# Final norm spread over the last two experts, its row loads on GpSimd's queue, the last six way-down quarters unsplit

## The chip, the cores and the metric

The kernel runs as one program on one core of a Trainium2 chip. The metric is the device time of an execution in microseconds; three runs of the kernel before are at hand, and one more execution was profiled. The engines are TensorE (PE), VectorE (DVE), ScalarE (ACT), GpSimd (POOL) and SyncE (SP, which only issues transfers). Each takes its instructions strictly in the order in which the scheduler has put them.

## The reference

Two transformer blocks on a sequence of 1024 rows of 1024 float32 numbers. Only the end of the second block matters here: 16 experts, each of which takes 128 rows, and a root-mean-square norm of the whole result.

```python
xs = jax.vmap(lambda hb, ib: hb[ib])(h, idx)                 # 128 rows for each expert
a = jnp.einsum('becd,edf->becf', xs, w_gate)
u = jnp.einsum('becd,edf->becf', xs, w_up)
y = jnp.einsum('becf,efd->becd', jax.nn.silu(a) * u, w_down) * g[..., None]
flat = (idx + (jnp.arange(bsz) * n)[:, None, None]).reshape(-1)
out = jax.ops.segment_sum(y.reshape(-1, d), flat, num_segments=bsz * n)
...
x = x + gt2 * out
return rmsnorm_2(x, g_final)     # x * rsqrt(mean(x*x) + EPS) * g_final, row by row
```

A row can be taken by several experts or by none.

## The kernel before

**Quarters.** Each expert's 1024 hidden columns are worked off in four quarters of 256, so there are 64 quarters, here numbered 0 to 63; expert 13 ends with quarter 55, expert 14 with 59, expert 15 with 63. A quarter q has three weight tiles of 1 MB: two with gate and up columns (gu q a and gu q b) and one of way-down rows (wd q). `pipelined` runs three stages, one step apart: `ex_gu(q)` (24 products into `pg`, then SiLU and a multiply into `sg`), `ex_T(q)` (two transposes into `pT`, copied out) and `ex_down(q)` (products into `py`, which collects the four quarters of an expert). So wd q is used two steps after gu q.

**Split weights.** The products run on pairs of float32r numbers: ACT casts half a tile (`wh`, line 1521), DVE subtracts (`wl`, line 1522), and `mm3` makes three products of each pair (lines 187 to 189). `wh` and `wl` have four buffers each, so the split is at most two tiles ahead of PE. Only the very last way-down quarter, 63, is multiplied unsplit (line 1739): four float32 products straight from the loaded tile, without a cast or a subtraction.

**Loads.** SP issues all weight loads in an order of its own queue, each as soon as the slot that it goes to is free. `raw_tile` hands out 17 slots of 1 MB in a fixed turn over six pools, so that a load runs up to 17 tiles ahead of its use. A split tile's slot is free when DVE has made its second `wl`.

**The end of an expert.** After its last quarter ACT scales `py` into `ys` (line 1745), POOL multiplies by a row (1746) and issues an indirect DMA that adds the 128 rows into `x3_d` in HBM (1750). For expert 14 DVE does both steps in one (1748), and all loads that are left are asked for there, the last three (wd 61, 62 and 63) behind POOL copies that read its `ys` (1498). Then `final_rows` loads the norm's weights `gfin` (1761), gathers expert 15's 128 rows (`xg`, 1763), loads all of `x3_d` into four slots of the same ring (`x3t`, two row tiles of 512 KB each, line 1770, on SP), and norms the eight row tiles: sum of squares on ACT (168), `vrstd` on DVE (161), a power on POOL (164), a scaling on DVE (1775) and a store to `out` on SP (1776). Expert 15's rows are added to `xg` in SBUF, normed on their own (lines 1786 to 1793), and put over the stored ones by an indirect DMA (1794).

**Order.** A list scheduler with its own estimate of times decides the order on each engine, so an instruction can stand ahead of one that was written before it. Tiles of one pool are placed in the order in which they are asked for.

Of the kernel before, what the change touches and what calls it, by code (L numbers as in the profile page):

```python
# [17 lines left out]
P = 128  # L18
# [45 lines left out]
LASTN = 3  # L64
# [30 lines left out]
def tile_two_blocks(ctx, tc, A, out):  # L95
# [51 lines left out]
    def trow(t):  # L147
        return slice(t * P, (t + 1) * P)
# [1490 lines left out]
    with TP(name="exg", bufs=2, space=PSUM) as psg, \  # L1639
# [69 lines left out]
        def ex_T(i, ac):  # L1709
            whole = i == 4 * NE - 1  # L1710
# [12 lines left out]
        def ex_down(i, a):  # L1723
            e, c4 = divmod(i, 4)
            whole = i == 4 * NE - 1
# [16 lines left out]
            if c4 == 3 and e < NE - 1:  # L1742
                ys = ex.tile([P, D], F32, name="ys", tag="xs", bufs=XSB)
                if e < NE - 2:
                    nc.scalar.activation(ys, py, AF.Copy, scale=xT[e][3])
                    nc.gpsimd.tensor_tensor(out=ys, in0=ys, in1=gt2, op=ALU.mult)
                else:
                    nc.vector.scalar_tensor_tensor(out=ys, in0=py, scalar=xT[e][3], in1=gt2,
                                                   op0=ALU.mult, op1=ALU.mult)
                nc.gpsimd.indirect_dma_start(out=x3_d, out_offset=bass.IndirectOffsetOnAxis(ap=xT[e][2], axis=0),  # L1750
                                             in_=ys, in_offset=None, compute_op=ALU.add)
                if e == NE - 2:
                    while order:
                        fetch(nc.sync, ys if len(order) <= LASTN else None)
                    final_rows()

        def final_rows():

            i_ = ROWS.index("g_final_2")
            last["g"] = ex.tile([P, D], F32, name="gfin", tag="xs", bufs=XSB)  # L1760
            nc.sync.dma_start(last["g"], A["rows"][i_:i_ + 1, :].partition_broadcast(P).rearrange("p o n -> p (o n)"))
            last["x"] = ex.tile([P, D], F32, name="xg", tag="xs", bufs=XSB)
            nc.gpsimd.indirect_dma_start(out=last["x"], out_offset=None, in_=x3_d,
                                         in_offset=bass.IndirectOffsetOnAxis(ap=xT[NE - 1][2], axis=0))
            for u in range(NT // 2):
                xt = raw_tile("x3t")
                for j in range(2):
                    t = 2 * u + j
                    x3 = xt[:, j * D:(j + 1) * D]
                    nc.sync.dma_start(x3, x3_d[trow(t), :])  # L1770
# [137 lines left out]
```

## Time and profile before

| | us |
|---|---|
| median of three runs (2452.44 to 2456.56) | 2456.46 |
| the profiled execution | 2458.82 |
| its span, first to last instruction | 2456.8 |
| PE busy over the span | 2329.6 |
| DVE busy over the span | 1609.7 |
| ACT busy over the span | 1123.5 |

A view groups or lists instructions of that one execution; times are counted from its first instruction. 2.0 us of the execution lie outside the span. Ends of matmuls are modelled, so the starts of PE's rows are the better clock. Idle time in square brackets stands with the engine and the operation that ended it.

### The profile page before, as it was taken

How to read it: one execution, taken by the hardware profiler on the slowest of the kernel's cores; microseconds unless marked ns; L12 is line 12 of the kernel's file. 1: busy time of each engine (PE TensorE's matmuls, PEld its weight loads, DVE VectorE, ACT ScalarE, POOL GpSimd, SP SyncE). 2: the span in 40 equal slices, each digit the busy share in tenths (PEclk: the TensorE clock that was granted, in tenths of full speed). 3: DMA queues.
4: the chain of work that ended last, by engine and by line, in shares of the span. 5: the costliest groups of instructions: out<-in, count | busy, mean ns of one | idle time of the engine just before them, and what ended most of it. 6: DMA issues, size and time to landing. Idle time of an engine off the chain costs nothing. (4 is left out here: it accounts for less than half of the span.)

```text
span 2456.8 us, 33997 instructions
## 1 busy us (share of the span) xinstructions
PE 2329.6 (95%) x12876; PEld 1876.7 (76%) x12876; DVE 1609.7 (66%) x2566; ACT 1123.5 (46%) x1933; POOL 606.6 (25%) x604
## 2 busy tenths in 40 slices
PE   7999999999999999999997999999959999999996
PEld 7977787787878878788876978666737888877774
DVE  4265666457686665454557742575377999999887
ACT  4254565343321222222223421453237887877775
POOL 1100540130000000000006400263164565565512
PEclk9999899999999999999998999999979999999998
DMA  5111003225243332111115220014778999999975
GB/s 199 30 48 57 24 27 99 97 99 162 83 156 103 120 103 65 47 52 43 52 54 144 88 64 26 26 40 144 236 286 335 383 381 379 397 361 366 367 256 214
DMA packets 111031, 381.66 MB, mean 155 GB/s; under 512 B 12215, under 2 KB 19224, under 8 KB 94484
## 3 DMA queue, kind: packets, MB, share of 16 engines
q1 hardware_dynamic: 98980, 344.99, 38.8%
q0 software_dynamic: 6416, 22.97, 4.0%
q10 hardware_dynamic: 5472, 11.54, 1.2%
q8 instruction: 101, 1.65, 0.3%
q14 instruction: 62, 0.51, 0.1%
HBM read 340.08 MB, written 39.37 MB: 154 GB/s over the span
## 5 line engine op out<-in xcount | busy, mean ns | idle before, releaser
L1522 DVE TENSOR_TENSOR wl<-raw,wh 128x1024 fp32r<-128x1024 f32 x378 | 469.1, 1277 | 45.2 <-ACT wh L1521 38.4
L1521 ACT CAST wh<-raw 128x1024 fp32r<-128x1024 f32 x382 | 391.2, 1051 | 69.0 <-PE pg L189 35.7
L171 ACT CAST wh<-raw 128x512 fp32r<-128x512 f32 (+1 forms) x177 | 107.5, 641 | 406.9 <-PE psu L188 221.3
L187 PE MATMUL psu<-hT_hi,wh 128*128 128x512 f32 x704 | 278.5, 396 | 5.5 <-ACT wh L171 5.3
L188 PE MATMUL psu<-hT_lo,wh 128*128 128x512 f32 x704 | 277.6, 395 | 0.0
L189 PE MATMUL psu<-hT_hi,wl 128*128 128x512 f32 x704 | 276.9, 395 | 0.2 <-DVE wl L172 0.2
L164 POOL TENSOR_TENSOR rrstd<-vrstd,neghalf 128x1 f32<-128x1 f32 x51 | 36.1, 731 | 866.6 <-DVE vrstd L161 866.5
L172 DVE TENSOR_TENSOR wl<-raw,wh 128x512 fp32r<-128x512 f32 (+1 forms) x177 | 124.1, 729 | 151.0 <-ACT wh L171 150.7
L888 DVE TENSOR_TENSOR ffn_y<-ffn_y,psd 128x512 f32<-128x512 f32 x160 | 108.5, 683 | 154.9 <-PE psd L189 154.7
L187 PE MATMUL pg<-wh,xh 128*128 128x512 f32 x512 | 204.5, 399 | 5.2 <-ACT xh L171 5.2
L1655 POOL TENSOR_SCALAR hot<-iota,slot 128x128 bf16<-128x128 f32 x112 | 204.2, 2557 | 16.2 <-PE pi L1663 16.1
L188 PE MATMUL pg<-wl,xh 128*128 128x512 f32 x512 | 204.0, 398 | 0.2 <-DVE wl L1522 0.2
L189 PE MATMUL pg<-wh,xl 128*128 128x512 f32 x512 | 202.2, 395 | 0.0
L187 PEld LDWEIGHTS psu<-hT_hi,wh 128*128 128x128 f32 x704 | 133.0, 189 | 37.9 <-ACT wh L171 8.1
L189 PEld LDWEIGHTS psu<-hT_hi,wl 128*128 128x128 f32 x704 | 132.9, 189 | 31.4 <-DVE wl L172 1.1
L188 PEld LDWEIGHTS psu<-hT_lo,wh 128*128 128x128 f32 x704 | 133.1, 189 | 30.0
L187 PE MATMUL psd<-wh,acth 128*128 128x512 f32 x352 | 140.0, 398 | 3.1 <-DVE ffn_y L888 2.9
L188 PE MATMUL psd<-wl,acth 128*128 128x512 f32 x352 | 139.1, 395 | 0.0
L189 PE MATMUL psd<-wh,actl 128*128 128x512 f32 x352 | 138.1, 395 | 0.0
L187 PEld LDWEIGHTS pg<-wh,xh 128*128 128x128 f32 x512 | 96.5, 188 | 25.9 <-ACT xh L171 7.1
L188 PEld LDWEIGHTS pg<-wl,xh 128*128 128x128 f32 x512 | 96.5, 188 | 24.4 <-DVE wl L1522 5.7
L189 PEld LDWEIGHTS pg<-wh,xl 128*128 128x128 f32 x512 | 96.3, 188 | 18.9
(498 smaller groups left out, 5411.1 us busy)
## 6 DMA issues: line engine op xcount, KB each, us to landing
raw<-in_w_gu SPq DMA_DIRECT2D x128, 1024.0 KB
raw<-in_w_down SPq DMA_DIRECT2D x64, 1024.0 KB
wa<-in_w_ada SPq DMA_DIRECT2D x48, 512.0 KB
raw<-in_w_up SPq DMA_DIRECT2D x88, 256.0 KB
raw<-in_w_down SPq DMA_DIRECT2D x44, 256.0 KB
raw<-in_w2t SPq DMA_DIRECT2D x36, 256.0 KB
xt<-in_x SPq DMA_DIRECT2D x16, 512.0 KB
wor<-in_w_out SPq DMA_DIRECT2D x32, 256.0 KB
```

The lines of the kernel that those rows point to most:

```text
L164: nc.gpsimd.tensor_tensor(out=r, in0=v, in1=neghalf[:, :n], op=ALU.pow)
L171: nc.scalar.copy(hi, src)
L172: nc.vector.tensor_tensor(out=lo, in0=src, in1=hi.bitcast(F32), op=ALU.subtract)
L187: nc.tensor.matmul(ps, lh, rh, start=start, stop=False)
L188: nc.tensor.matmul(ps, lh, rl, start=False, stop=False)
L189: return nc.tensor.matmul(ps, ll, rh, start=False, stop=stop)
L888: nc.vector.tensor_tensor(out=yt, in0=yt, in1=ps, op=ALU.add)
L1521: nc.scalar.copy(wh, raw[:, sl])
L1522: (eng or nc.vector).tensor_tensor(out=wl, in0=raw[:, sl], in1=wh.bitcast(F32), op=ALU.subtract)
L1655: nc.gpsimd.tensor_scalar(hot[:, t, :], iota1, slot_of[e][:, t, :], None, op0=ALU.is_equal)
```

## The change

The row loads for the final norm move from behind expert 14 to behind expert 13: there POOL issues expert 13's scatter, a gather of expert 14's rows, and then itself the eight loads of `x3_d` into the four `x3t` tiles. SP issues `gfin`, now a whole slot of the ring with room for one normed result. So five of the ring's slots go to the norm before quarter 58's weights are asked for. Expert 14's rows are treated as expert 15's were: `add_rows` adds them to the gathered rows and sums the squares, `norm_rows` norms them and scatters them over `out`; they are also written to `x3_d`, for expert 15's gather. `final_rows(u)` norms the two row tiles of `x3t` u, and is called in the way-down stages of quarters 58 to 61. Quarters 58 to 63 (`WHOLE = 6`) are multiplied unsplit. `LASTN` and the copies that held the last three loads back are gone.

```diff
--- before.py
+++ after.py
@@ -61,7 +61,8 @@
 ONORM = (26, 29)
 MORE = 2
 XSB = 3
-LASTN = 3
+WHOLE = 6
+FROWS = {58: 0, 59: 1, 60: 2, 61: 3}
 OH = 1
 KV0 = 1
 D1S = 3
@@ -1707,7 +1708,7 @@
             return sg
 
         def ex_T(i, ac):
-            whole = i == 4 * NE - 1
+            whole = i >= 4 * NE - WHOLE
             pT = pst.tile([P, 4, P], F32, name="pT", tag="tp")
             for j in range(2):
                 nc.tensor.transpose(pT[:, j, :], ac[:, j * P:(j + 1) * P], ident)
@@ -1722,7 +1723,7 @@
 
         def ex_down(i, a):
             e, c4 = divmod(i, 4)
-            whole = i == 4 * NE - 1
+            whole = i >= 4 * NE - WHOLE
             ah, al = a
             if c4 == 0:
                 pys[e] = psy.tile([P, D], F32, name="py", tag="y")
@@ -1741,58 +1742,75 @@
                         mm3(py[:, c], ah[:, j, :], al[:, j, :], *part(w, cw_.start, 512), start, stop)
             if c4 == 3 and e < NE - 1:
                 ys = ex.tile([P, D], F32, name="ys", tag="xs", bufs=XSB)
+                idx = bass.IndirectOffsetOnAxis(ap=xT[e][2], axis=0)
                 if e < NE - 2:
                     nc.scalar.activation(ys, py, AF.Copy, scale=xT[e][3])
                     nc.gpsimd.tensor_tensor(out=ys, in0=ys, in1=gt2, op=ALU.mult)
+                    nc.gpsimd.indirect_dma_start(out=x3_d, out_offset=idx, in_=ys, in_offset=None, compute_op=ALU.add)
+                    if e == NE - 3:
+                        last["x"] = rows_of(e + 1)
+                        gn = raw_tile("gfin")
+                        last["g"], last["n"] = gn[:, 0:D], gn[:, D:2 * D]
+                        i_ = ROWS.index("g_final_2")
+                        nc.sync.dma_start(last["g"],
+                                          A["rows"][i_:i_ + 1, :].partition_broadcast(P).rearrange("p o n -> p (o n)"))
+                        last["t"] = [raw_tile("x3t") for _ in range(NT // 2)]
+                        for t in range(NT):
+                            nc.gpsimd.dma_start(last["t"][t // 2][:, t % 2 * D:t % 2 * D + D], x3_d[trow(t), :])
                 else:
-                    nc.vector.scalar_tensor_tensor(out=ys, in0=py, scalar=xT[e][3], in1=gt2,
-                                                   op0=ALU.mult, op1=ALU.mult)
-                nc.gpsimd.indirect_dma_start(out=x3_d, out_offset=bass.IndirectOffsetOnAxis(ap=xT[e][2], axis=0),
-                                             in_=ys, in_offset=None, compute_op=ALU.add)
-                if e == NE - 2:
-                    while order:
-                        fetch(nc.sync, ys if len(order) <= LASTN else None)
-                    final_rows()
-
-        def final_rows():
-
-            i_ = ROWS.index("g_final_2")
-            last["g"] = ex.tile([P, D], F32, name="gfin", tag="xs", bufs=XSB)
-            nc.sync.dma_start(last["g"], A["rows"][i_:i_ + 1, :].partition_broadcast(P).rearrange("p o n -> p (o n)"))
-            last["x"] = ex.tile([P, D], F32, name="xg", tag="xs", bufs=XSB)
-            nc.gpsimd.indirect_dma_start(out=last["x"], out_offset=None, in_=x3_d,
-                                         in_offset=bass.IndirectOffsetOnAxis(ap=xT[NE - 1][2], axis=0))
-            for u in range(NT // 2):
-                xt = raw_tile("x3t")
-                for j in range(2):
-                    t = 2 * u + j
-                    x3 = xt[:, j * D:(j + 1) * D]
-                    nc.sync.dma_start(x3, x3_d[trow(t), :])
-                    jk = ex.tile([P, D], BF16, name="jk", tag="hot", bufs=1)
-                    ss = stat.tile([P, 1], F32, name="ss", tag="ss")
-                    sumsq(x3, ss, jk)
-                    r = rstd_of(ss, 1, D)
-                    nc.vector.scalar_tensor_tensor(out=x3, in0=x3, scalar=r, in1=last["g"], op0=ALU.mult, op1=ALU.mult)
-                    nc.sync.dma_start(out[trow(t), :], x3)
+                    add_rows(e, ys)
+                    nc.gpsimd.indirect_dma_start(out=x3_d, out_offset=idx, in_=ys, in_offset=None)
+                    last["x"] = rows_of(e + 1)
+                    last["y"] = ys
+            if i in FROWS:
+                final_rows(FROWS[i])
+            if i == 4 * NE - 3:
+                norm_rows(NE - 2, last["y"], last["n"])
+
+        def rows_of(e):
+
+            xg = ex.tile([P, D], F32, name="xg", tag="xs", bufs=XSB)
+            nc.gpsimd.indirect_dma_start(out=xg, out_offset=None, in_=x3_d,
+                                         in_offset=bass.IndirectOffsetOnAxis(ap=xT[e][2], axis=0))
+            return xg
+
+        def add_rows(e, ys):
+            last["sq"] = stat.tile([P, 2], F32, name="ssl", tag="ssl")
+            jk = ex.tile([P, D], BF16, name="jk", tag="hot", bufs=1)
+            for nh in range(2):
+                c = slice(nh * 512, nh * 512 + 512)
+                nc.vector.scalar_tensor_tensor(out=ys[:, c], in0=pys[e][:, c], scalar=xT[e][3], in1=gt2[:, c],
+                                               op0=ALU.mult, op1=ALU.mult)
+                nc.vector.tensor_tensor(out=ys[:, c], in0=ys[:, c], in1=last["x"][:, c], op=ALU.add)
+                sumsq(ys[:, c], last["sq"][:, nh:nh + 1], jk[:, c])
+
+        def norm_rows(e, ys, to):
+
+            ss = stat.tile([P, 1], F32, name="ss", tag="ss")
+            nc.vector.tensor_tensor(out=ss, in0=last["sq"][:, 0:1], in1=last["sq"][:, 1:2], op=ALU.add)
+            r = rstd_of(ss, 1, D)
+            nc.vector.scalar_tensor_tensor(out=to, in0=ys, scalar=r, in1=last["g"], op0=ALU.mult, op1=ALU.mult)
+            nc.gpsimd.indirect_dma_start(out=out, out_offset=bass.IndirectOffsetOnAxis(ap=xT[e][2], axis=0),
+                                         in_=to, in_offset=None)
+
+        def final_rows(u):
+
+            xt = last["t"][u]
+            for j in range(2):
+                t = 2 * u + j
+                x3 = xt[:, j * D:(j + 1) * D]
+                jk = ex.tile([P, D], BF16, name="jk", tag="hot", bufs=1)
+                ss = stat.tile([P, 1], F32, name="ss", tag="ss")
+                sumsq(x3, ss, jk)
+                r = rstd_of(ss, 1, D)
+                nc.vector.scalar_tensor_tensor(out=x3, in0=x3, scalar=r, in1=last["g"], op0=ALU.mult, op1=ALU.mult)
+                nc.sync.dma_start(out[trow(t), :], x3)
 
         pipelined(4 * NE, ex_gu, ex_T, ex_down)
 
-
         ys = ex.tile([P, D], F32, name="ys", tag="xs", bufs=XSB)
-        sq = stat.tile([P, 2], F32, name="ssl", tag="ssl")
-        jk = ex.tile([P, D], BF16, name="jk", tag="hot", bufs=1)
-        for nh in range(2):
-            c = slice(nh * 512, nh * 512 + 512)
-            nc.vector.scalar_tensor_tensor(out=ys[:, c], in0=pys[NE - 1][:, c], scalar=xT[NE - 1][3], in1=gt2[:, c],
-                                           op0=ALU.mult, op1=ALU.mult)
-            nc.vector.tensor_tensor(out=ys[:, c], in0=ys[:, c], in1=last["x"][:, c], op=ALU.add)
-            sumsq(ys[:, c], sq[:, nh:nh + 1], jk[:, c])
-        ss = stat.tile([P, 1], F32, name="ss", tag="ss")
-        nc.vector.tensor_tensor(out=ss, in0=sq[:, 0:1], in1=sq[:, 1:2], op=ALU.add)
-        r = rstd_of(ss, 1, D)
-        nc.vector.scalar_tensor_tensor(out=ys, in0=ys, scalar=r, in1=last["g"], op0=ALU.mult, op1=ALU.mult)
-        nc.gpsimd.indirect_dma_start(out=out, out_offset=bass.IndirectOffsetOnAxis(ap=xT[NE - 1][2], axis=0),
-                                     in_=ys, in_offset=None)
+        add_rows(NE - 1, ys)
+        norm_rows(NE - 1, ys, ys)
     for p in reversed(exs):
         p.release()
     rt_pool.release()
```

The scheduler's order changes from about quarter 55 on. SP before, with the tiles' own numbers: wd 55, the two tiles of gu 58, wd 56, and the two of gu 59.

```order
L1500 DMA raw_21352<-in_w_down2 128x2x1024
L1503 DMA raw_21379<-in_w_gu 128x2048
L1503 DMA raw_21401<-in_w_gu 128x2048
L1500 DMA raw_21434<-in_w_down2 128x2x1024
L1503 DMA raw_21457<-in_w_gu 128x2048
L1503 DMA raw_21479<-in_w_gu 128x2048
```

SP of the changed kernel, from wd 58 (raw_21616) on: behind it stand the two tiles of gu 61 and wd 59 (raw_21693), then gu 58 (raw_21395 and raw_21417) and wd 56 (raw_21450), then gu 63 b, wd 61 and wd 62.

```order
L1501 DMA raw_21616<-in_w_down2 128x2x1024
L1504 DMA raw_21641<-in_w_gu 128x2048
L1504 DMA raw_21663<-in_w_gu 128x2048
L1501 DMA raw_21693<-in_w_down2 128x2x1024
L1504 DMA raw_21395<-in_w_gu 128x2048
L1504 DMA raw_21417<-in_w_gu 128x2048
L1501 DMA raw_21450<-in_w_down2 128x2x1024
L1504 DMA raw_21830<-in_w_gu 128x2048
L1501 DMA raw_21860<-in_w_down2 128x2x1024
L1501 DMA raw_21897<-in_w_down2 128x2x1024
L1807 DMA out_0<-x3t_21382 128x1024 x2
```

Gu 58 and wd 56 moved behind the loads of gu 59 to wd 59. They come from the pool of the last `x3t` tile, behind it; and wd 59 goes to the slot of wd 55.

ACT before, from expert 13's `ys` into quarter 59's casts: raw_21401 is gu 58 b, raw_21434 wd 56, raw_21457 gu 59 a.

```order
L1745 ACTIVATE ys_21374<-py_21089,gate_20417 128x1024
L1521 CAST wh_21407<-raw_21401 128x1024
L1521 CAST wh_21436<-raw_21434 128x1024
L171 CAST ah_21429<-pT_21426 128x256
L1521 CAST wh_21440<-raw_21434 128x1024
L1521 CAST wh_21459<-raw_21457 128x1024
L1705 ACTIVATE sg_21423<-pg_21378 128x256
L1521 CAST wh_21463<-raw_21457 128x1024
```

ACT of the changed kernel in the same place: raw_21395 and raw_21417 are gu 58, raw_21450 wd 56, raw_21473 gu 59 a; `sg_21439` is quarter 58's.

```order
L1747 ACTIVATE ys_21374<-py_21089,gate_20417 128x1024
L172 CAST ah_21445<-pT_21442 128x256
L1522 CAST wh_21397<-raw_21395 128x1024
L1522 CAST wh_21401<-raw_21395 128x1024
L1522 CAST wh_21419<-raw_21417 128x1024
L1522 CAST wh_21423<-raw_21417 128x1024
L1522 CAST wh_21452<-raw_21450 128x1024
L1522 CAST wh_21456<-raw_21450 128x1024
L169 ACTIVATE jk_21622,ss_21623<-x3t_21382 128x1024
L1522 CAST wh_21475<-raw_21473 128x1024
L169 ACTIVATE jk_21631,ss_21632<-x3t_21382 128x1024
L1706 ACTIVATE sg_21439<-pg_21394 128x256
```

Two sums of squares of the first `x3t` tile moved in, one ahead of the first cast of gu 59 and one ahead of quarter 58's SiLU.

SP before, its end, without numbers: gu 63 and `gfin`, the last three way-down tiles, row loads and stores.

```order
L1503 DMA raw<-in_w_gu 128x2048 x2
L1761 DMA gfin<-in_rows 128x1024
L1500 DMA raw<-in_w_down 128x2x1024 x3
L1770 DMA x3t<-x_d 128x1024 x8
L1776 DMA out<-x3t 128x1024 x8
```

SP of the changed kernel, its end: raw_21730 and raw_21752 are gu 62 a and b, raw_21783 is wd 60, raw_21808 gu 63 a, raw_21903 wd 63.

```order
L1504 DMA raw_21730<-in_w_gu 128x2048
L1504 DMA raw_21752<-in_w_gu 128x2048
L1501 DMA raw_21783<-in_w_down2 128x2x1024
L1807 DMA out_0<-x3t_21383 128x1024 x2
L1807 DMA out_0<-x3t_21384 128x1024 x2
L1504 DMA raw_21808<-in_w_gu 128x2048
L1807 DMA out_0<-x3t_21385 128x1024 x2
L1501 DMA raw_21903<-in_w_down2 128x2x1024
```

The stores moved between the last weight loads. In the built program raw_21730, raw_21752 and raw_21783 have one and the same slot, which the first `x3t` tile had before them, and raw_21808 has that of the second, x3t_21383.

## Rows read from the trace of the kernel before

**Rows 1.** Chain that ended last, its last 157 us: start us, us, what

```profile
2419.32 10.67 DMA x3t<-x_d
```

**Rows 2.** Table of stretches: length, each engine's busy time (instructions), PE clock, DMA share, GB/s

```profile
2380.00:2390.00 10.00, 10.00 (x49) 8.25 (x47) 10.00 (x12) 7.94 (x9) 0.00 (x0) 1.00 0.23 43
```

**Rows 3.** Groups by form, last 157 us: busy us, mean ns | idle before

```profile
L1522 DVE TENSOR_TENSOR wl<-raw,wh 128x1024 fp32r<-128x1024 f32 x83 | 102.8, 1271 | 12.8 <-ACT wh L1521 10.6
L1521 ACT CAST wh<-raw 128x1024 fp32r<-128x1024 f32 x82 | 84.6, 1050 | 16.7 <-PE pg L189 7.8 <-PE py L189 5.0 <-DMA raw<-in_w_down 3.0
L1775 DVE SCALAR_TENSOR_TENSOR x3t<-x3t,rrstd,gfin 128x1024 f32<-128x1024 f32 x8 | 10.2, 1281 | 2.8 <-POOL rrstd L164 2.8
L168 ACT ACTIVATE jk<-x3t 128x1024 bf16<-128x1024 f32 x8 | 8.5, 1057 | 4.1 <-DMA x3t<-x_d 3.4
L172 DVE TENSOR_TENSOR al<-pT,ah 128x256 fp32r<-128x256 f32 x14 | 5.8, 418 | 1.0 <-ACT ah L171 1.0
L164 POOL TENSOR_TENSOR rrstd<-vrstd,neghalf 128x1 f32<-128x1 f32 x9 | 7.3, 817 | 19.1 <-DVE vrstd L161 19.1
L1788 DVE TENSOR_TENSOR ys<-ys,xg 128x512 f32<-128x512 f32 x2 | 1.3, 682 | 0.0
L168 ACT ACTIVATE jk<-ys 128x512 bf16<-128x512 f32 x2 | 1.2, 622 | 0.0
```

**Rows 4.** PE in order of time: start us, us, line, operation

```profile
2371.88 0.39 PE L189 MATMUL py<-wh,al 128*128 128x512 f32 x1
2372.11 0.39 PE L188 MATMUL pg<-wl,xh 128*128 128x512 f32 x1
2379.75 0.39 PE L187 MATMUL pg<-wh,xh 128*128 128x512 f32 x1
2431.52 3.67 PE L1739 MATMUL py<-raw,af 128*128 128x512 f32 x8 [0.31 <-issue]
```

**Rows 5.** DVE in order of time

```profile
2367.63 2.59 DVE L1522 TENSOR_TENSOR wl<-raw,wh 128x1024 fp32r<-128x1024 f32 x2 [0.39 <-ACT wh L1521]
2437.26 1.41 DVE L1786 SCALAR_TENSOR_TENSOR ys<-py,gate,mod 128x512 f32<-128x512 f32 x2
```

**Rows 6.** ACT in order of time

```profile
2421.90 1.05 ACT L1521 CAST wh<-raw 128x1024 fp32r<-128x1024 f32 x1 [2.72 <-DMA raw<-in_w_down]
```

**Rows 7.** POOL in order of time

```profile
2376.24 2.29 POOL L1750 DMA_INDIRECT x_d<-ys,idx  x1 [0.28 <-POOL ys L1746]
2419.53 2.01 POOL L1763 DMA_INDIRECT xg<-x_d,idx  x1 [2.90 <-DMA x_d<-ys,idx]
2450.59 1.05 POOL L1794 DMA_INDIRECT out<-ys,idx  x1 [2.69 <-DMA out<-x3t]
```

**Rows 8.** Landings: expert 13's scatter; all transfers on x3_d; eight earlier loads by POOL

```profile
DMA to landing us min/median/max: 7.7/7.7/7.7
DMA to landing us min/median/max: 6.9/8.9/10.6
L949 POOL DMA_DIRECT2D ffn_y<-x_d x8: 877/882/940, 1295.7 to 1353.4; - x8
DMA to landing us min/median/max: 5.5/5.6/6.1
```

**Rows 9.** SP's issues in order of time: start us, us from the first to the last

```profile
2390.28 0.33 SPq L1761 DMA_DIRECT2D gfin<-in_rows  x1
2414.70 2.33 SPq L1500 DMA_DIRECT2D raw<-in_w_down  x3
2419.32 9.23 SPq L1770 DMA_DIRECT2D x3t<-x_d  x8
```

**Rows 10.** Table of stretches of 0.5 us, around the transfer of gfin

```profile
2391.00:2391.50 0.50, 1.00 0.38 139
```

**Rows 11.** Table of stretches of 1 us, an earlier place where PE waited

```profile
559.00:560.00 1.00, 0.90 (x3) 0.50 0.97 360
564.00:565.00 1.00, 1.00 (x4) 0.63 1.07 410
```

## The prediction, made before the changed kernel was run

> **What bounds the kernel now.** I read the chain that ended last from its end, then the tables of stretches, then each engine in order of time around expert 13's end and the kernel's end. Up to the last way-down quarter the end is set by PE and by the split that feeds it: from 2380 to 2390 PE is busy 10.00 us of 10 and DVE 10.00 too [rows 2]. The split costs 1.27 us of DVE and 1.05 us of ACT for each half tile [rows 3], so a tile takes DVE 2.5 us, and a quarter of three tiles 7.6 us. Anything put on DVE here delays PE. The weights are far ahead: the transfers use 0.23 of the DMA engines there, 43 GB/s. PE's last product ends at 2431.52 + 3.67 = 2435.2 [rows 4], and the span at 2456.8. The 21.6 us between are the final norm: loads of `x3_d` that landed 10.67 us after their issue [rows 1], eight sums and norms, the stores, and expert 15's scatter, issued at 2450.59 [rows 7]. The change takes up most of these 21.6 us. What it can gain is bounded by that; what it can lose is decided where its loads meet a full pipeline.
>
> **The part that is removed.** After PE's last product only expert 15's own rows remain: two scalings 1.41 [rows 5], two additions 1.36, a half sum of squares 0.62, a power 0.82, a norm 1.28 [rows 3], about 0.5 for the two tiny DVE operations and 0.6 of hand-overs (estimates), and the scatter from issue to the end, 2456.8 - 2450.59 = 6.2 [rows 7]. Sum 12.8 against 21.6: **8.8 us are saved**, if PE ended where it does.
>
> **Unsplit quarters.** A way-down quarter is 12 products of 0.23 (start to start, 2371.88 to 2372.11), 2.8 us of PE; unsplit it takes 3.67 [rows 4]. Five more quarters: 5 x 0.9 = +4.5 us of PE. Each takes 2.5 us from DVE and 2.1 from ACT, which pays for the eight norms and sums. PE loses more than nothing only where DVE was not the limit; I count PE's time below.
>
> **First wait: gu 58 behind wd 59.** On SP gu 58 is now behind wd 59, and wd 59 goes to the slot of wd 55, so it can't be issued before wd 55's second split, at 2367.63 + 1.3 = 2368.9 [rows 5]. A load's first bytes move 0.9 us after its issue (`gfin` issued at 2390.28, moving within 2391.0 to 2391.5) [rows 9, 10], and a full DMA moves 410 GB/s [rows 11], 2.5 us for 1 MB. Wd 59, then gu 58 a: 2369.1 + 0.4 + 0.9 + 2 x 2.5 = 2375.4. PE runs out of products at about 2372 (the last `py` of expert 13 is at 2371.88): it idles 3 to 4 us. From above the landing is bounded by 7.2 us, the first of the three held-back way-down tiles (2414.70 to 2421.90) [rows 6, 9]: 2376.7. This wait is swallowed by the next one.
>
> **Second wait: ACT behind the row loads.** In ACT's order the sum of squares of the first `x3t` tile stands ahead of gu 59's first cast. Behind it on ACT are that cast, quarter 58's SiLU and all further splits, so PE and DVE wait for it. The chain to it: expert 13's scatter is issued at 2376.0 (before 2376.24 [rows 7]; `ys` a little earlier, since ACT has no casts ahead of it), lands 7.7 us later as before (6.9 to 10.6 for transfers on these rows [rows 8]), 2383.7; POOL then issues the gather of expert 14's rows, 2.0 us [rows 7], and 0.2, 2385.9; then the first row load, 5.6 us as eight earlier loads from POOL took [rows 8], and 1.3 for the gather's 0.5 MB ahead of it, 2392.8. Sum 1.06, cast 1.05 [rows 3]: gu 59's first product at 2394.9. Before it ran at 2379.75 [rows 4]: **+15.2 us**. From below 6.9 and 3.4 (0.9 + 2.5) give 2390.6, +10.9; from above 10.6 and 6.1 + 2.5 give 2399.5, +19.8. A gain is excluded, since no scatter landed in under 6.9. I take the middle, from the same scatter and the nearest loads. That POOL rather than SP issues the eight loads costs 0.88 us each [rows 8] against the 0.33 of `gfin` on SP (eight in a row took SP 9.23, with waits for slots) [rows 9]: 4.4 us over eight, on an idle engine; the first load sees 0.5 of it.
> The Trainium skill ("DMA: Bandwidth & Descriptors", section Anatomy of one DMA — SWDGE (gpsimd) path) fits a transfer issued by GpSimd as 2.0 us and the bytes by 436 GB/s: an estimate of 3.2 us for 512 KB, where the row has 5.6 [rows 8]; by it the sum would be 3.7 us less. The measured landing is taken. The Trainium skill ("Trainium Kernel Development and Optimization", section Key Constraints) says that transfers issued from SP, ACT and GpSimd run on the same 16 engines, and that another issuer saves only the issue time; by that rule the move of the loads to GpSimd's queue gives the weights no way around them.
>
> **From there to gu 62 b.** Quarter 59 is now DVE's: four splits 5.1, two norms 2.6, `al` and `sg` 0.8, small ones 0.3, 8.8 us, and six products behind the last split, 1.4: 2405.1. Then PE has 72 products (quarter 57's 12 `py`, gu 60, 61 and 62 a), 16.6, two unsplit quarters, 7.3, and transposes, 0.9: 24.8 us, 2429.9. Gu 62 a, gu 62 b and wd 60 have one and the same slot, so gu 62 b is issued when gu 62 a has been split, some 4 us before PE has finished it, and a load takes 3.4 (0.9 + 2.5) to 7.2: **0.2 us** of waiting, at most 3.2. Its products can start at 2430.1.
>
> **Third wait: gu 63 a behind the stores.** Gu 63 a goes to the second `x3t` tile's slot, and stands on SP behind the stores of the third, so it waits for four norms. ACT and DVE first have gu 62 b's split: 1.05 + 2 x 1.27 = 3.6; then four norms, 5.1, and 2.4 for powers (0.82 each, partly hidden), vrstd and `sg` (estimate): issued at 2430.1 + 11.1 = 2441.2. Landing 5.3 (0.9, 2.5, and 1 MB of stores ahead, some 2; 3.4 to 7.2 as bounds): 2446.5. Queued behind it are the stores of the last tile and wd 63, but those are not needed before 2458. Its first product follows the cast, at 2447.5. PE has gu 62 b, 12 x 0.23, and wd 60 and wd 61, 3.67 each, to do until then, 10.1 of 17.4 us: **7 us** lost.
>
> **The end.** First cast 1.05, four splits 5.1, six products 1.4: 2454.0. Wd 62 3.67, transposes and hand-over 0.9, wd 63 3.67: PE ends at 2462.3. And 12.8: 2475.1. Against the span's 2456.8 that is +18.3 us. The profiled execution's own time is 2458.82, 2.0 outside the span and 2.4 above the median; on the median of 2456.46 it gives **2475 us**.
>
> **Rivals.**
> A. The rows come sooner: the scatter in 6.9, the first load in 3.4. For it: the DMA is nearly idle at 2380 to 2390 [rows 2]. Against: expert 13's own scatter took 7.7 in that quiet stretch, and the loads by POOL never under 5.5 [rows 8]. Time: 2475 - 4.3, and less in the third wait (5.3 becomes 3.4): 2467 to 2469.
> B. PE's clock falls after each wait. At an earlier place where PE waited about 4 us the granted clock was 0.50 (1.2 GHz) at 559 and still 0.63 in the microsecond from 564 [rows 11], so some 3 us of PE's time were lost by the slower clock. Two or three such waits (4, 12 and 7 us) cost up to 3 x 3 us, less where DVE is the limit: 2480 to 2484. For it: the waits here are longer. Against: DVE is the limit just behind the second.
> C. Faster, by the waits not being there: ACT's sums find their rows landed and gu 63 a is in time. Then PE ends at 2435.2 + 4.5, less some 2 us of small stalls in which DVE's lighter load helps, and with the tail of 12.8 the span is about 2450.5, a median of 2450, -0.3%. It decides if all waits together cost less than 6.3 us (8.8 - 4.5 + 2); the rows give 15.2 for the second alone, 10.9 at the least. For it: all loads of the last tiles stand earlier than before, so that the 2.72 us that ACT waited for wd 61 [rows 6] go. Against: ACT stands behind the first sum in the built program.
> D. The second wait hides the first and A's rows hold, and gu 63 a lands in time, so that no third wait is left: 2461 less some 2 us, within 2452 to 2461, no difference.
>
> **How the numbers follow.** A measurement of this kernel tells about 0.2%, 4.9 us, from no change. Chances: the forecast (2469 to 2481) 0.45; B (2480 to 2488) 0.25; A (2461 to 2469) 0.17; C 0.07; D 0.06. The sum of the bounds goes from +10.9 + 0 for the third wait's low end (2463) to +19.8 + 3 + 2 (2482), and B's clock 6 to 8 more: the range 2460 to 2490 leaves out C, most of D and a little of either end. Slower has 0.45 + 0.25 + 0.17 = 0.87, same 0.06, faster 0.07.
>
> **What would show it.** In the changed profile: PE idle from about 2372 to 2375, ended by gu 58's cast after its DMA; ACT idle until about 2393 ahead of the first sum of squares, released by the DMA of `x3t`, and gu 59's first product near 2395 (wrong if under 2388); gu 62 b's cast with little wait; a wait of some 7 us ahead of gu 63 a's first cast, its load issued behind the third tile's stores at about 2441; PE's last product at about 2462, and 12 to 14 us from there to the end. Granted clock near 1.00 behind the waits speaks against B, 0.50 for it. If the sum of squares on ACT finds its rows already landed, or gu 63 a's load stands earlier than the norms, the forecast is wrong.

## The result, and the profile after

The changed kernel takes 2479.84 us, the median of four runs (2476.16 to 2483.11), beside 2456.51 us for four runs of the kernel before: a ratio of 1.0094, with a 95% interval of 1.0076 to 1.0112. It is slower by 23 us. Its profiled execution took 2478.43 us, with a span of 2476.7, against 2458.82 and 2456.8 before: 19.9 us more in span. That pair of profiles is what the steps below are read from.

The two executions are not level where the change begins. Quarter 56's first product, ahead of the first wait, stands here before and after:

```profile
2353.50 0.50 PE L187 MATMUL pg<-wh,xh 128*128 128x512 f32 x1 [0.75 <-ACT xh L171]
2347.19 0.50 PE L188 MATMUL pg<-wh,xh 128*128 128x512 f32 x1 [0.75 <-ACT xh L172]
```

The changed kernel's execution has a lead of 6.3 us there. The change did not make it: the order of work differs from about quarter 55 on, and expert 8's scatter, long before that, is already issued at 2198.63 against 2204.96. From quarter 56's first product to the end of the span it takes 129.5 us against 103.3, so like for like its end is 26.2 us longer. A time of the changed profile is comparable with a time before, or with a forecast made from it, after 6.3 us are added.

TensorE in order of time, from quarter 58 on (start us, us, line, operation; in brackets the idle time ahead and what ended it; only the four longest waits, and the last quarter):

```profile
2371.21 0.80 PE L188 MATMUL pg<-wh,xh 128*128 128x512 f32 x1 [4.30 <-ACT wh L1522]
2391.78 0.79 PE L188 MATMUL pg<-wh,xh 128*128 128x512 f32 x1 [8.74 <-ACT wh L1522]
2431.72 0.58 PE L1714 MATMUL pT<-ident,sg 128*128 128x128 f32 x2 [2.75 <-DVE vrstd L162]
2445.81 0.80 PE L188 MATMUL pg<-wh,xh 128*128 128x512 f32 x1 [4.82 <-ACT wh L1522]
2460.21 3.70 PE L1740 MATMUL py<-raw,af 128*128 128x512 f32 x8 [0.52 <-ACT af L1717]
```

Before, quarter 59's first product ran at 2379.75 [rows 4]; here it is the row at 2391.78, which is 2398.1 on the clock of the profile before. Of the four waits three were forecast; the one at 2431.72 was not. PE ends at 2460.21 + 3.70 = 2463.9, and 12.8 us later the span is over.

What the first two and the last wait hang on, on ScalarE:

```profile
2370.11 1.99 ACT L1522 CAST wh<-raw 128x1024 fp32r<-128x1024 f32 x2 [2.91 <-DMA raw<-in_w_gu]
2389.65 1.06 ACT L169 ACTIVATE jk<-x3t 128x1024 bf16<-128x1024 f32 x1 [11.09 <-DMA x3t<-x_d]
2444.71 3.89 ACT L1522 CAST wh<-raw 128x1024 fp32r<-128x1024 f32 x4 [10.95 <-DMA raw<-in_w_gu]
```

The 11.09 us at 2389.65 are the first sum of squares waiting for its rows, with quarter 59's first cast behind it. GpSimd shows the chain ahead of that, and what comes before the wait that was not forecast:

```profile
2369.64 1.61 POOL L1749 DMA_INDIRECT x_d<-ys,idx  x1 [0.28 <-POOL ys L1748]
2379.07 1.59 POOL L1773 DMA_INDIRECT xg<-x_d,idx  x1 [7.83 <-DMA x_d<-ys,idx]
2380.67 3.80 POOL L1759 DMA_DIRECT2D x3t<-x_d  x7
2426.92 1.23 POOL L1773 DMA_INDIRECT xg<-x_d,idx  x1 [3.12 <-DMA x_d<-ys,idx]
2428.17 1.10 POOL L165 TENSOR_TENSOR rrstd<-vrstd,neghalf 128x1 f32<-128x1 f32 x2
```

The gather of expert 15's rows (2426.92) waits 3.12 us for expert 14's scatter, and the powers of the norm are queued behind it; DVE has two norms behind those powers, and `sg` behind the norms. The gather's own part is small: the first power's input was there at 2427.34, and it started at 2428.17, 0.8 us later; the two norms take 2.5 us. The loads on SyncE: wd 59 and the two tiles of gu 58, and further on gu 63 a:

```profile
2362.57 0.38 SPq L1501 DMA_DIRECT2D raw<-in_w_down  x1
2363.00 0.94 SPq L1504 DMA_DIRECT2D raw<-in_w_gu  x2
...
2437.00 0.34 SPq L1504 DMA_DIRECT2D raw<-in_w_gu  x1
2437.39 0.90 SPq L1807 DMA_DIRECT2D out<-x3t  x2
```

Rows of the chain that ended last (start us, us, what):

```profile
2380.67 8.89 DMA x3t<-x_d
2426.92 1.23 POOL xg L1773
2428.17 0.60 POOL rrstd L165
2431.30 5.63 DMA out<-x3t
2437.00 7.68 DMA raw<-in_w_gu
```

And the table of stretches around the waits (length, busy time of PE, PEld, DVE, ACT, POOL, PE's granted clock, DMA share, GB/s):

```profile
2376.00:2377.00 1.00, 1.00 (x4) 0.76 (x3) 0.05 (x1) 0.97 (x1) 0.00 (x0) 0.50 1.07 213
2380.00:2390.00 10.00, 3.04 (x14) 2.10 (x12) 0.00 (x0) 0.35 (x1) 5.00 (x9) 0.88 1.02 412
2396.00:2397.00 1.00, 1.00 (x5) 0.95 (x4) 1.00 (x2) 0.82 (x1) 0.00 (x0) 0.50 1.02 410
2398.00:2399.00 1.00, 1.00 (x6) 0.78 (x5) 1.00 (x2) 0.50 (x1) 0.00 (x0) 1.00 0.94 377
```

Where 2380 to 2390 was PE 10.00, DVE 10.00 and 43 GB/s before [rows 2], and the stretch that is level with it, 2386.3 to 2396.3, PE 8.61, DVE 8.33 and 52 GB/s, PE is now busy for 3.04 us, DVE for none, and the transfers run at 412 GB/s. After each of the three longer waits PE's granted clock is 0.50 (1.2 GHz) for about six microseconds of products; after the 2.75 us at 2431.72 it is 0.50 too, from 2432 to 2435.

### The profile page after: what moved, and what is told of

Read it like the earlier page. It is cut to its first block, busy times and chain, and to the rows that moved or that the text cites. A ratio compares the mean times of both kernels' runs of the same rounds, so it can differ in the third digit from the quotient of the medians.

```text
span 2476.7 us, 33923 instructions
## 1 busy us (share of the span) xinstructions
PE 2337.1 (94%) x12856; PEld 1875.4 (76%) x12856; DVE 1597.6 (65%) x2557; ACT 1113.1 (45%) x1927; POOL 607.0 (25%) x612
## 5 line engine op out<-in xcount | busy, mean ns | idle before, releaser
L1523 DVE TENSOR_TENSOR wl<-raw,wh 128x1024 fp32r<-128x1024 f32 x368 | 455.8, 1276 | 60.1 <-ACT wh L1522 55.0
L1522 ACT CAST wh<-raw 128x1024 fp32r<-128x1024 f32 x372 | 380.1, 1051 | 85.2 <-PE pg L190 41.6
L190 PEld LDWEIGHTS pg<-wh,xl 128*128 128x128 f32 x512 | 98.5, 192 | 19.8 <-issue 0.5
```

The source lines that it names most:

```text
L190: return nc.tensor.matmul(ps, ll, rh, start=False, stop=stop)
L1522: nc.scalar.copy(wh, raw[:, sl])
L1523: (eng or nc.vector).tensor_tensor(out=wl, in0=raw[:, sl], in1=wh.bitcast(F32), op=ALU.subtract)
```

## The experiments

All runs beside the kernel before on the same chip; times are medians, ratios those to the kernel before with their 95% intervals. The last column is the one profiled execution: the time from quarter 56's first product to the end of the span, which leaves out what differs ahead of the change. It is 103.3 us for the kernel before.

| | us | ratio | interval | from quarter 56 on |
|---|---|---|---|---|
| changed kernel | 2479.84 | 1.0094 | 1.0076 to 1.0112 | 129.5 |
| e1, split again | 2482.15 | 1.0096 | 1.0077 to 1.0116 | 134.6 |
| e2, unsplit alone | 2455.85 | 1.0003 | 0.9989 to 1.0016 | 105.2 |
| e3, rows at once | 2468.79 | 1.0047 | 1.0030 to 1.0063 | 117.9 |
| e4, slots asked for at 58 | 2455.72 | 0.9999 | 0.9985 to 1.0012 | 103.0 |
| e5, three tiles first | 2458.94 | 1.0015 | 1.0003 to 1.0028 | 107.2 |
| e6, norm one stage later | 2490.58 | 1.0136 | 1.0115 to 1.0157 | 132.7 |
| e7, e5 with loads on SyncE | 2458.42 | 1.0015 | 1.0002 to 1.0028 | 107.1 |
| e8, e4 with a direct add | 2457.75 | 1.0006 | 0.9994 to 1.0019 | 105.4 |
| e9, e5 without row slots | 2452.32 | 0.9988 | 0.9974 to 1.0003 | 101.3 |
| e10, e9 with sums spread | 2449.24 | 0.9978 | 0.9964 to 0.9991 | 98.0 |
| e11, e10, four unsplit | 2449.05 | 0.9968 | 0.9954 to 0.9983 | 97.4 |

### Are the unsplit quarters to blame?

e1 takes them out of the changed kernel; e2 puts them alone into the kernel before.

```diff
-WHOLE = 6
+WHOLE = 1
```

> The changed kernel with only the last way-down quarter unsplit, as before (the limit of 6 back to 1). Theory A (three waits behind the row loads cost the time, the unsplit quarters next to nothing): PE gets back 5 x 0.9 = 4.5 us, ACT and DVE get 5 x 2.1 and 5 x 2.5 us more in stretches that wait anyway, so the time stays within 4 us of the changed kernel's 2479.8, and the three waits are still there. Rival B (the unsplit products are what makes it slower): at least 5 us less, under 2475.

> The kernel before with the last six way-down quarters unsplit, nothing else. Theory A: its end is set by the row loads behind expert 14 and by the norms, not by PE, and ACT and DVE have 2.1 and 2.5 us less for each of five quarters, so the time is within 4 us of 2456.5. Rival B: 4.5 us or more are added, 2461 or above.

Both came as theory A had it: 1.0096 against the changed kernel's 1.0094, and 1.0003. The first two waits of e1 are the same (4.22 and 8.44 us of idle PE ahead of quarters 58 and 59); its later ones come to 13.7 us (3.17, 1.86, 5.15 and 3.48) against 7.6, in an execution that is the longest of its six. The 4.5 us of PE that five more unsplit quarters cost don't show in e2's time; its chain that ended last goes through 11.03 us of row loads, as before [rows 1]. Rival B is out.

### Is it the rows' lateness, or the norm's own work?

e3 loads rows that are there already (the kernel's input rows, so that the values normed are not those of the reference).

```diff
+                if e == NE - 3:
+                    ...                     # slots and loads, now ahead of expert 13's scatter
-                            nc.gpsimd.dma_start(..., x3_d[trow(t), :])
+                        nc.gpsimd.dma_start(..., A["x"][trow(t), :])
```

> The changed kernel with row loads that wait for nothing: they read the kernel's input rows instead of the summed rows, and stand ahead of expert 13's scatter; so the values normed are not those of the reference. In the built program quarter 58's weights are then loaded in their turn, and the first sum of squares stands far ahead of expert 13's end; the weights of quarters 62 and 63 still go to the slots of the first two row tiles. Theory A: the first two waits go (4.3 and 8.7 us of PE idle, and 2 to 4 us of slow clock behind them), the third stays: 2462 to 2467. Rival C (what costs is the norm's own work beside the last quarters, wherever its rows come from): 2473 or above.

2468.8 us: 11 us of the 23 are gone, less than A forecast (2462 to 2467) and more than C (2473). The first two waits are gone: PE is busy 9.57 and 10.00 us of 10 from 2370 and from 2380 on. What A missed is further on:

```profile
2410.00:2420.00 10.00, 6.44 (x19) 3.59 (x17) 6.84 (x11) 7.45 (x15) 2.30 (x2) 0.83 0.25 54
2420.00:2430.00 10.00, 0.80 (x1) 0.29 (x1) 3.27 (x7) 5.21 (x8) 4.13 (x5) 0.61 0.77 266
```

(columns as above.) From 2419.0 to 2431.9 PE makes one product. First it waits 5.37 us for gu 62 b, which goes to the slot of gu 62 a and is issued at 2416.69, when that tile has been split. Then it waits 6.71. The table of waits (engine, line, what it waited for: us in total, times, longest) and GpSimd in order of time say why:

```profile
PE pg L189 <- DVE wl L1523: 9.2, 5, 6.7
DVE x3t L1807 <- POOL rrstd L165: 8.0, 4, 6.4
...
2424.81 1.00 POOL L1774 DMA_INDIRECT xg<-x_d,idx  x1 [6.50 <-DMA x_d<-ys,idx]
```

GpSimd stands ahead of the gather of expert 15's rows for 6.5 us, the powers behind it keep a norm on DVE for 6.4, and the split behind that norm keeps PE for 6.7. The same order, with a shorter hold, stands ahead of the changed kernel's wait at 2431.72. So C has a share in it, by the norm's order on the engines and not by its amount.

### Is it the slots?

In the changed kernel gu 58 stands behind the last row tile in one pool of the ring. e4 moves the place where the five slots are asked for to the head of quarter 58's way-down stage, where they fill a pool of one and a pool of four.

```diff
-FROWS = {58: 0, 59: 1, 60: 2, 61: 3}
+FROWS = {59: 0, 60: 1, 61: 2, 62: 3}
...
             py = pys[e]
+            if i == 58:
+                gn = raw_tile("gfin")
+                ...
             raw = wload("w_down2", i)
```

> The changed kernel with the five slots of the norm asked for, and the rows loaded, at the head of quarter 58's way-down stage instead of at expert 13's end, where the five tiles fill one small pool and one whole pool, so that no weight tile stands behind a row tile in its pool; and the four row tiles are normed one stage later each. Eleven weight tiles are left then, for twelve slots, so that no weights go to a slot of the rows. Theory A: all three waits go; PE ends at about 2437 to 2441 and 12.8 us follow, 2450 to 2456 in all, no slower than before. Rival C: 2465 or above, since the same sums, norms, and unsplit products are all still there.

2455.7 us, ratio 0.9999. (Its last row tile is stored behind expert 14's normed rows, so that those rows of the output hold old values.) From 2364 on PE's rows show no load wait; it ends at 2434.90 + 3.70 = 2438.6, in the forecast 2437 to 2441. But 20 us follow, and not 12.8. GpSimd and DVE in order of time:

```profile
2436.20 1.55 POOL L1763 DMA_INDIRECT x_d<-ys,idx  x1 [0.18 <-issue]
2441.20 1.04 POOL L1774 DMA_INDIRECT xg<-x_d,idx  x1 [2.23 <-DMA x_d<-ys,idx]
2445.85 1.29 DVE L1785 TENSOR_TENSOR ys<-ys,xg 128x512 f32<-128x512 f32 x2 [3.56 <-DMA xg<-x_d,idx]
```

Expert 14's scatter now stands behind seven powers of the norm, and expert 15's addition waits for the gather behind it. All waits ahead of PE's end are away, and the gain went into a new one behind it.

e8 frees that scatter of the gathered rows (it adds in HBM, as in the kernel before), and puts the sums and powers behind it; expert 14's normed rows come last again.

```diff
-                    add_rows(e, ys)
-                    nc.gpsimd.indirect_dma_start(out=x3_d, out_offset=idx, in_=ys, in_offset=None)
+                    ...                     # ys = py * gate * gt2
+                    last["i"] = nc.gpsimd.indirect_dma_start(out=x3_d, out_offset=idx, in_=ys, in_offset=None, compute_op=ALU.add)
...
+                with tc.issue_after(last["i"].ins):
                     sumsq(x3, ss, jk)
                     r = rstd_of(ss, 1, D)
```

> As e4 (slots asked for at the head of quarter 58's way-down stage, row tiles normed one stage later), with expert 14's rows added into HBM by the scatter itself, so that the scatter doesn't wait for the gathered rows, and the sums and powers of the norm put behind that scatter; expert 14's rows are put over the result behind the last row tile. In e4 that scatter was issued at 2436.2 and the gather behind it ended expert 15's wait at 2445.85. Theory A: the scatter is issued by 2415 and the gather lands by 2440, about where PE ends (2438); then 12.8 to 15.4 us follow: 2450 to 2454 in span, 2 to 5 us less than the kernel before. Rival: another load or store at the end takes the gap, and it stays within 2 us of 2455.5.

The scatter is issued at 2414.62, as forecast, and PE ends at 2436.8; still the time is 1.0006. The norms had moved too:

```profile
2431.74 1.28 DVE L1819 SCALAR_TENSOR_TENSOR x3t<-x3t,rrstd,gfin 128x1024 f32<-128x1024 f32 x1
2440.30 1.40 DVE L1794 SCALAR_TENSOR_TENSOR ys<-py,gate,mod 128x512 f32<-128x512 f32 x2
2452.56 0.96 POOL L1805 DMA_INDIRECT out<-ys,idx  x1 [3.15 <-DMA out<-gfin,idx]
```

The first norm is at 2431.74, so that DVE reaches expert 15's scaling 3.5 us after PE's end, and the last scatter waits for the one of expert 14. By the ratio the rival was right; what took the gap was the norms' place on DVE.

### One line: three tiles first

e5 leaves the place and asks for quarter 58's three tiles before the five slots.

```diff
                         last["x"] = rows_of(e + 1)
+                        for _ in range(3):
+                            fetch(nc.sync)
                         gn = raw_tile("gfin")
```

> The changed kernel with one thing moved: the three tiles of quarter 58 (two of gate and up, and the way-down tile 56) are asked for just ahead of the five slots of the norm instead of just behind them, so that the four row tiles fill one pool of four slots and nothing stands behind them in it until the next turn of the ring. In the built program quarter 58 is then loaded in its turn, and the first sum of squares moves back behind the casts of quarter 62; the last tiles still go to the slots of the row tiles. Theory A2 (the place in the ring is the one cause of the first two waits, since the sums' place on ACT follows from when the planner sees quarter 58's weights arrive): both waits go, 4.3 and 8.7 us of PE idle and 2 to 4 us of slow clock, and a third of 3 to 7 us stays ahead of quarter 63: 2456 to 2465. Rival (the wait on expert 13's rows is met wherever the sums stand): above 2470.

2458.9 us: the ratio falls from 1.0094 to 1.0015, and with it 19 of the 23 us are back. Both waits are gone, though every sum, norm, row load and unsplit product is as it was. So the first two waits come from one place in the program, the turn of the ring: with gu 58 back in its place, the planner also put the first sum behind the casts of gu 62 a. What is left is one wait, on PE and SyncE:

```profile
2426.74 0.79 PE L188 MATMUL pg<-wh,xh 128*128 128x512 f32 x1 [10.63 <-ACT wh L1522]
2417.13 0.39 SPq L1504 DMA_DIRECT2D raw<-in_w_gu  x1
```

Gu 63 b has the slot of the first row tile: it waits for that tile's stores, stands on SyncE behind three stores of later tiles, too, and is issued at 2417.13. Its first cast starts at 2425.65, 8.15 us after ACT's work before it.

e7 is e5 with the row loads on SyncE.

```diff
-                            nc.gpsimd.dma_start(last["t"][t // 2][:, t % 2 * D:t % 2 * D + D], x3_d[trow(t), :])
+                            nc.sync.dma_start(last["t"][t // 2][:, t % 2 * D:t % 2 * D + D], x3_d[trow(t), :])
```

> As the kernel with three tiles first (e5), with the eight row loads issued by SyncE instead of GpSimd. In the built program they then stand on SyncE behind way-down tile 60 and ahead of quarter 63's weights. By the Trainium skill (Trainium Kernel Development and Optimization, section Key Constraints) the issuing engine saves issue time only; by that rule this should be within 2 us of e5. Theory A2: the rows land later, since SyncE reaches them only when the slots of quarters 61 and 62 have come free, about 2400 instead of 2385, and the sums behind them on ACT wait: 3 to 10 us slower than e5.

2458.4 us, and the same ratio of 1.0015. My expectation (3 to 10 us slower) was wrong: SyncE issued them from 2381.04 on, where GpSimd does in e5 from 2384.52 on. The Trainium skill (Trainium Kernel Development and Optimization, section Key Constraints) says that transfers issued from SP, ACT and GpSimd run on the same 16 engines, and that issuing from several of them saves only issue time; the two runs agree with it, 2458.94 and 2458.42 us.

### The second wait by itself

e6 keeps the slots of the changed kernel and norms each tile one stage later (59 to 62); expert 14's rows follow one stage later, too.

> The changed kernel with each row tile normed one way-down stage later (59 to 62 instead of 58 to 61; expert 14's own rows are put over the result one stage later too), the slots as in the changed kernel. In the built program all sums of squares stand behind the casts of quarter 61, and quarter 58's weights still behind way-down tile 59. Theory A2: the first wait stays (PE idle 4 to 5 us near 2367), the second goes (8.7 us and the slow clock), the third grows, since quarter 62's first tile now waits for three stores: 2466 to 2476. If the time stays within 2477 to 2483, the second wait was not on the path.

The second wait is gone: from 2380 to 2410 PE is busy 10.00 of 10. The first is still there (4.19 us). But the third is far longer than I had said:

```profile
2371.26 0.79 PE L188 MATMUL pg<-wh,xh 128*128 128x512 f32 x1 [4.19 <-ACT wh L1522]
2429.35 0.79 PE L188 MATMUL pg<-wh,xh 128*128 128x512 f32 x1 [17.41 <-ACT wh L1522]
2439.32 0.80 PE L188 MATMUL pg<-wh,xh 128*128 128x512 f32 x1 [3.65 <-ACT wh L1522]
```

Now quarter 62's first tile waits for the row tiles' stores, with all eight sums ahead of its casts, and the kernel takes 2490.6 us, some 10 more than the changed one by the two ratios. (The profiled execution is the shortest of the five, 2481.86 us, and 3.2 us more by the last column.) The two waits are not two costs to be added: shifting the norm only moves the place where weights and rows meet in one slot.

### No weights in the rows' slots

e9 is e5 with a ring that passes over the norm's slots from then on (12 slots for the last weights); e10 also holds about the order on ScalarE that e5 had; e11 has four unsplit quarters in place of six.

```diff
+        if turn[1] and turn[0] % len(spots) == 5:
+            turn[0] += 5
         pool, n = spots[turn[0] % len(spots)]
...
-                w = ahead.pop(("w_gu", 2 * i + hf), None) or wsplit(wload("w_gu", 2 * i + hf))
+                w = ahead.pop(...) or wsplit(wload(...), first=last.get({(62, 1): ("s", 0), (63, 0): ("s", 1), (63, 1): ("s", 2)}.get((i, hf))))
```

(`first`: the casts are issued after that sum. The second piece is in e10 and e11, not in e9.)

> As e5 (three tiles first), and the ring passes over the five slots of the norm from then on, so that no weight tile goes to a slot of the rows. In the built program the weights of quarter 63 and the last way-down tiles are loaded in their turn; all sums of squares move behind the last cast on ACT, as in e4. Theory A: the third wait (10.6 us of PE idle ahead of quarter 63's second tile in e5, and its slow clock) goes, PE ends at about 2432 to 2436; but as in e4 the norms and expert 14's scatter then stand late, and 18 to 20 us follow: 2450 to 2456 in all. Rival: the norms fit beside the last products, 12.8 us follow: 2445 to 2449.

> As e9, with the planner told to put the casts of quarter 62's second tile and of quarter 63's two tiles behind the sums of the first, second and third row tile on ACT, which is about where those sums stand in e5. Theory A: no load waits, and the norms are done before PE is: PE ends at 2432 to 2437, then 12.8 us: 2445 to 2451, 5 to 10 us less than the kernel before. Rival: ACT and DVE have not the room beside the last splits, and PE waits for them: 2454 or above.

> As e10, with only the last four way-down quarters unsplit instead of six. PE gets back 2 x 0.9 us, ACT and DVE have 2 x 2.1 and 2 x 2.5 us more, both before the norms begin. Theory A: within 2 us of e10.

e9 takes 2452.3 us (0.9988, the interval includes 1): no load wait is left and PE ends at 2426.95 + 3.70 = 2430.7, but the span ends 18.8 us later, at 2449.5. As in e4 the gather of expert 15's rows is late (it lands at 2438). e10 takes 2449.2 us, 0.9978 with an interval under 1: **it is faster than both kernels**, by 5 us against the kernel before. Its chain that ended last (start us, us, what) has nothing behind PE but expert 15's own rows:

```profile
2433.14 0.63 issue
2433.77 0.74 DVE ys L1792
2437.02 0.57 POOL rrstd L165
2437.59 1.36 issue
2438.95 1.26 POOLq L1932
```

PE ends at 2429.37 + 3.70 = 2433.1, and 12.7 us later the span ends at 2445.8, as the 12.8 of the prediction. The waits inside are small (1.54 us at most). e11 is 0.9968, and its interval overlaps e10's: four or six unsplit quarters can't be told apart. The intervals of e9 and e10 overlap, too; that the order on ScalarE helped is read from the chain, where the late gather is gone, and not shown by the times.

## Why the prediction was right, step by step

The forecast of 2475 us, slower, lies 4.8 us under the median, and its mechanism was there: weights behind late rows on SyncE, ScalarE behind the first sum of squares, gu 63 a behind the stores. Its sizes were too small. From quarter 56 on the end grew by 26.2 us where 18.3 were forecast (the medians differ by 23.3). Against the profiled span it lies only 1.6 us off (2475.1 for 2476.7), and that is luck: this execution had its lead of 6.3 us before the change had any part in it. Below, these 6.3 us are taken off the forecast's times, until the sum.

- **What the norm's move saves** (8.8 us, a tail of 12.8): measured 2476.7 - 2463.9 = 12.8 in the changed kernel, 12.8 in e5 (2456.5 - 2443.7) and 12.7 in e10. Right.
- **The unsplit quarters** (counted at PE's time, a cost only where DVE isn't the limit): e1 and e2 put them at nothing in either kernel. The single product block took 3.70 us, as in rows 4.
- **The first wait** (3 to 4 us from 2365.7, gu 58 behind wd 59): 4.30 us from 2366.9, released by gu 58's transfer. Wd 59 was issued at 2362.57, where the forecast has 2362.8. Gu 58 took 7.1 us from issue to its first cast (2363.00 to 2370.11), near the upper bound of 7.2. Right, at the upper end.
- **"Swallowed by the next one"**: right in the sum. The chain that ended last goes from the scatter through the first row load to the sum, and not through gu 58. What I did not see is that one place in the ring makes both: e5 lost both by one edit, and e6 has the first without the second.
- **The second wait** (+15.2 us, first product of quarter 59 at 2388.6): 2391.78, which is +18.3, within the bounds of 10.9 and 19.8. The scatter was issued as forecast (2369.64 for 2369.7). The chain behind it was mis-sized, 2391.78 - 2369.64 = 22.1 against 18.9: scatter to gather 9.4 where I took 7.7, gather to first load 1.6 where I took 2.2, first load to sum 9.0 where I took 6.9. My row for the scatter had 70 GB/s of transfers beside it; here the scatter has 335 GB/s and the first load 412. For the first load the 3.2 us that the Trainium skill's fit gave as an estimate (DMA: Bandwidth & Descriptors, section Anatomy of one DMA — SWDGE (gpsimd) path) are further off than the row that I took.
- **Gu 62 b** (0.2 us, for its load): its first product came at 2425.27 without a wait, and the next one waited 0.44 us for DVE's subtraction, none of it for the load.
- **A wait that I had not seen**: 2.75 us at 2431.72, by two norms ahead of `sg` on DVE, some 0.8 of it by the gather on GpSimd's queue. I moved the gather past SyncE's and ACT's queues in thought, but not past the powers on its own engine. PE would have waited for gu 63 a in any case; what counts is that the chain that ended last goes through that gather, a power, a norm, a store and gu 63 a.
- **The stretch between** (from quarter 59's first product to gu 62 b's, 35.2 us): 33.5, from 2391.78 to 2425.27, 1.7 less.
- **The third wait** (gu 62 b's first product to gu 63 a's, 17.4 us, 7 of them lost; issue 11.1 after gu 62 b): 20.5 us, from 2425.27 to 2445.81, 3.1 more; PE lost 2.75 + 4.82 = 7.6. The issue came 11.7 after gu 62 b (at 2437.00). The landing was the mis-sized term: 7.7 (2437.00 to 2444.71) where I took 5.3, over the upper bound of 7.2, with the stores of two row tiles ahead, and two more stores right behind.
- **Rival B, the clock**: its mechanism is there. After 2371.21 and 2445.81 ten or eleven products each are 0.43 us apart instead of 0.23, some 2.1 us each; after 2391.78 and 2431.72 the clock is 0.50 as well. I had left it out of the sum. Behind the last wait it is paid in full: from gu 63 a's first product to PE's end I had 14.8 us, and it took 18.1, 3.3 more. Of these, 2.6 lie in the 24 products, of which DVE's splits were done at 2450.42 and PE at 2454.9, and 0.7 in a second hand-over ahead of the last two quarters, where I had counted one.
- **The sum**: against the forecast PE's end stands at +3.2 (second wait) - 1.7 + 3.1 (third) + 3.3 (the end) = +7.9 us, less the lead of 6.3: +1.6, 2463.9 for 2462.3, and the span with it. Three terms were too small and one too large.
- **Rival C, faster**, asked for all waits together to cost under 6.3 us. The changed kernel never came near it. e10, in which those waits are gone, gives about the time that C had worked out: 2449.2 for 2450.

## What to carry to other kernels

When tiles that wait for something late are taken from a ring that the planner fills in order, what comes behind them in the same pool waits too, in the planner's order if not in its data: take them where they fill a pool, and keep the ring's next turn off their slots until they are done. A change that takes work off the tail should be costed by where its loads and its queue entries meet the full pipeline, and each moved instruction has to be followed through the queue of its own engine. A gain can go from one wait to the next several times (e4, e6, e8): look at the last chain again after each fix. And two profiles are compared from an instruction that stands ahead of the change in both: here 6.3 us between them had nothing to do with it.

## What the runs showed of the hardware that was not expected

Expert 13's scatter of 128 rows, the same instruction each time, landed 7.7 us after its issue in the kernel before [rows 8], with 70 GB/s of transfers over that time, 9.2 in the changed kernel with 335 GB/s, and 10.9 in e5 with 238 GB/s: the bytes beside it alone don't set the order, and the cause stays open. Expert 14's scatter, which writes its rows without adding them, landed after 3.4 us in the changed kernel and in e1, and after 8.7 in e3. A 512 KB load that GpSimd issued took 9.0 us until its reader started, with the transfers at 412 GB/s, against 5.6 from issue to landing [rows 8], with 110 to 251 GB/s in the stretches around those loads. After idle PE times of 2.75, 4.30, 4.82 and 8.74 us the granted clock was 0.50 in the rows that follow (until 2435, 2377, 2452 and 2397); at e10's longest wait, 1.54 us, it stayed at 1.00. And the 512 KB loads of all `x3t` tiles, from one issuing engine or the other, cost the kernel the same (1.0015 of the kernel before in e5 and in e7).
